# The FFN's down-projection: four passes over 22 chunks, or seven products over 11 pairs of chunks

## The chip, the cores and the metric

The kernel runs on one core of a Trainium2 chip. The metric is the device time of one execution in microseconds (us), the median of several runs. The engines are PE (TensorE, the matmuls; PEld is its weight loads), DVE (VectorE), ACT (ScalarE), POOL (GpSimd) and SP (SyncE, which here issues the transfers by DMA).

## The reference

One layer of a hybrid encoder, on 2048 tokens of 1024 channels in float32. Attention and pooling come first; the change concerns the second half of the layer, with DFF = 2816:

```python
def conv_ffn(x, conv_w, conv_b, w_up, w_down):
    h = x @ w_up
    h = lax.conv_general_dilated(h, conv_w[:, None, :], window_strides=(1,),
                                 padding=[(CONV_WIDTH - 1, 0)],
                                 dimension_numbers=('NWC', 'WIO', 'NWC'),
                                 feature_group_count=2 * D_FF) + conv_b
    gate, val = jnp.split(h, 2, axis=-1)
    return (jax.nn.silu(gate) * val) @ w_down
...
        ffn = conv_ffn(x, conv_w[l], conv_b[l], w_ffn_up[l], w_ffn_down[l])
        x = layer_norm(ALPHA * x + ffn, ln2_g[l], ln2_b[l])
```

## The kernel before

A float32 product is emulated: each operand is split into `hi` (rounded to fp32r, on ACT) and `lo` (the rest, on DVE or POOL), and `mm3` issues three matmuls, hi·hi, hi·lo and lo·hi. Tokens are worked on in two halves of 1024. `ffn` (L1669) runs `up_half(0)`, `down_half(0)`, `up_half(1)`, `down_half(1)` one after the other.

**Up-projection.** `up_half` (L1463) has 22 units of 7 steps: each unit makes 256 channels, for 1024 tokens, by seven products of sums and differences of blocks (`ORDER`), 12 matmuls in a step. Evacuations add and subtract the products from PSUM into small tiles (`m`, eight buffers of 2 KB a partition). Two units in a row are gate and value of the same channels; a pair of units yields two chunks of h. Beside the next unit run the steps of `conv` (L1501): two multiply-adds per chunk on DVE, and in `hidden` (L1526) the product with the gate, after which the chunk of 128 channels x 1024 tokens (512 KB) goes to `self.store`; `turn` (L346) issues it on SP a step later (L353). In the first half, POOL and ACT also build the block sums of the up weights (`up_weights`), stored by the same way and fetched with `up_fetch` (L1459). DVE also makes sums of x (`x_mix`, L1409).

**Down-projection.** `down_half` (L1594) runs four passes per token half: two quarters of 512 tokens (q) by two halves of the outputs (c), each over the 22 chunks of h (k), so 88 steps. A step loads a block of h and a block of the weights, 256 KB each, into the two halves of one tile (`down_load`, L1579, transfers at L1582 and L1583), splits it in `down_split` (L1585), and issues 12 matmuls, three for each of four token blocks of 128 rows, which add up in four PSUM banks (`p1`). Loads run one step ahead of the split, splits two steps ahead of the matmuls; the first three loads and two splits are made in the last unit of the up-projection. After a pass, DVE adds each bank into a tile y that came from memory (512 KB, L1640); after c = 1 the tile is normed (`norm_stages`: ACT sums, DVE and POOL small operations, two DVE operations of 128x1024) and stored. In the fourth pass of the first half, `x_load`, `x_turn` and `x_mix` of the second half are called by a table in `ffn` (`ahead_up`, steps 1 to 21 of the pass). The last six chunks of the very last pass are held and worked off bank by bank.

The Tile framework gives out the buffers (`b`: 42 of 4 KB a partition, `m`: 8 of 2 KB, PSUM `p1`: 4 banks, `p2`: two pairs of banks) and the waits; on each engine instructions run in the order in which they were placed. Every engine instruction passes a helper that counts work, so its line in the profile is L140 and tiles tell the instructions apart; transfers keep their own lines.

## Time and profile before

| | us |
|---|---|
| median of 3 runs | 3350.85 (3349.14 to 3353.66) |
| profiled execution, its own time | 3344.69 |
| its span, first to last instruction | 3342.9 |
| mean granted TensorE clock, share of full | 0.984 |
| first up-projection, by the trace | 1960 to 2403 |
| first down-projection | 2403 to 2666 |
| second up-projection | 2666 to 3087 |
| second down-projection | 3087 to 3343 |

A time of the profiled execution is set against 3344.69, not against the median. Busy shares overlap, since the engines run side by side; an engine's idle time costs something only where a later one waits for it. PE's matmuls are pipelined, so the distance between their starts counts, not the length of one.

### The profile page before, as it was taken

Reading aid. Unit: us, or ns where it says so; the run is one execution under the profiler, and the core shown is the slowest. Engines: PE = TensorE matmul, PEld = TensorE weight load, DVE = VectorE, ACT = ScalarE, POOL = GpSimd, SP = SyncE. Lnnn points to the kernel's source line nnn. Section 1 sums busy time; section 2 is a strip of 40 time slices with the busy share of each in tenths; the row PEclk is TensorE's granted clock in tenths of the full one; section 3 lists DMA queues with packets and bytes.
Section 4 is the critical chain, followed back from the end, with each engine's and each line's share of the span. In section 5 each row is a group of like instructions: output and inputs, shape, how many; then the busy total and the mean of one; then the engine's idle time right before and its main releaser. Section 6 shows DMA issues by size and latency. Waiting matters only on the chain.

```text
span 3342.9 us, 47116 instructions
## 1 busy us (share of the span) xinstructions
PE 3213.2 (96%) x16182; PEld 2703.1 (81%) x16182; DVE 2326.4 (70%) x4378; ACT 1606.5 (48%) x2876; POOL 1208.8 (36%) x1269
## 2 busy tenths in 40 slices
PE   8998899999999899999999989999999999999998
PEld 8887688888898788888788877778788788888787
DVE  5589878996899887777676665565555755555655
ACT  3455837855777666666511133332354522223542
POOL 3139400010011786766631165440185500000754
PEclk9999899999999999999999999999999999999999
DMA  8457755753665444344464378986587466655763
GB/s 322 145 196 277 258 196 199 252 186 136 225 248 186 138 168 160 142 167 154 162 219 154 127 259 322 333 330 221 208 291 238 158 239 232 225 210 208 268 219 130
DMA packets 300334, 711.11 MB, mean 213 GB/s; under 512 B 27258, under 2 KB 112190, under 8 KB 300094
## 3 DMA queue, kind: packets, MB, share of 16 engines
q1 hardware_dynamic: 290302, 690.26, 57.9%
q10 hardware_dynamic: 9792, 17.83, 1.4%
q8 instruction: 128, 2.10, 0.3%
q14 instruction: 112, 0.92, 0.1%
HBM read 497.06 MB, written 210.93 MB: 212 GB/s over the span
## 4 chain that ended last, share of the span: by engine, by line
PE 55%; DVE 5%; issue 2%; POOL 1%; ACT 1%; DMA 1%; SPq 0%; POOLq 0%; DVEq 0%; ACTq 0%
PE p L140 55%; DVE b L140 4%; ACT b L140 1%; DVE m L140 1%; POOL b L140 1%; DMA b<-in_w_ffn_down_dram 0%; DMA h<-b 0%; DMA b<-uw 0%; ACT m L140 0%; POOL lt L140 0%; POOL nr L140 0%; POOL l L140 0%; POOL lr L140 0%; POOL lv L140 0%; DVE nt L140 0%
## 5 line engine op out<-in xcount | busy, mean ns | idle before, releaser
L140 PE MATMUL p<-b,b 128*128 128x512 f32 (+2 forms) x12820 | 2843.3, 369 | 65.5 <-ACT b L140 21.8
L140 PEld LDWEIGHTS p<-b,b 128*128 128x128 f32 x12820 | 2206.4, 191 | 471.6 <-ACT b L140 23.9
L140 POOL TENSOR_TENSOR b<-b,b 128x512 fp32r<-128x512 f32 (+3 forms) x408 | 529.4, 1318 | 690.2 <-DMA b<-x 408.1
L140 ACT ACTIVATE b<-p 128x512 fp32r<-128x512 f32 (+9 forms) x726 | 428.5, 612 | 652.3 <-PE p L140 617.7
L140 ACT ACTIVATE b<-b 128x1024 fp32r<-128x1024 f32 (+2 forms) x270 | 275.8, 1029 | 354.3 <-DMA b<-in_w_ffn_down_dram 138.0
L140 ACT ACTIVATE m<-b,F 128x448 bf16<-128x448 f32 (+3 forms) x448 | 366.0, 819 | 80.7 <-DVE F L140 70.8
L140 DVE TENSOR_TENSOR b<-b,b 128x512 fp32r<-128x512 f32 (+4 forms) x268 | 320.0, 1220 | 102.4 <-ACT b L140 78.9
L140 DVE TENSOR_SCALAR_CACHE_REDUCE m<-b,F 128x512 bf16<-128x512 f32 (+6 forms) x476 | 370.9, 809 | 15.5 <-DMA q<-m 10.6
L140 DVE TENSOR_TENSOR m<-m,p 128x512 f32<-128x512 f32 x176 | 120.6, 685 | 271.4 <-ACT b L140 207.0
L140 PE MATMUL p<-b 128*128 128x512 f32 x704 | 271.3, 390 | 0.4 <-DVE b L140 0.4
L140 DVE SCALAR_TENSOR_TENSOR b<-b,cw,b 128x1023 f32<-128x1023 f32 (+1 forms) x176 | 248.4, 1413 | 30.6 <-ACT b L140 28.9
L140 POOL TENSOR_SCALAR b<-b 128x256 fp32r<-128x256 f32 (+3 forms) x216 | 117.7, 559 | 370.6 <-DMA b<-in_w_in_dram 168.1
L140 DVE TENSOR_TENSOR b<-p,b 128x512 fp32r<-128x512 f32 (+1 forms) x286 | 201.5, 713 | 60.1 <-ACT b L140 57.8
L140 PE MATMUL p<-ident,b 128*128 128x128 f32 x1456 | 213.7, 275 | 20.8 <-ACT b L140 14.2
L140 DVE CUSTOM_DVE_ANT_0 b<-p,b 128x1024 f32<-128x1024 f32 (+7 forms) x192 | 174.0, 908 | 67.0 <-PE p L140 65.5
L140 PEld LDWEIGHTS p<-ident,b 128*128 128x128 f32 x1456 | 175.4, 142 | 53.7 <-ACT b L140 17.5
L140 ACT ACTIVATE b<-b,mx 128x1024 f32<-128x1024 f32 (+7 forms) x192 | 171.6, 896 | 67.7 <-DVE mx L140 63.4
L140 ACT ACTIVATE m<-p 128x512 f32<-128x512 f32 (+1 forms) x180 | 105.5, 594 | 177.8 <-PE p L140 164.7
L140 DVE SCALAR_TENSOR_TENSOR b<-b,ws,b 128x768 f32<-128x768 f32 (+5 forms) x154 | 157.4, 1050 | 41.7 <-ACT b L140 39.4
L140 PEld LDWEIGHTS p<-b 128*128 128x128 f32 x704 | 132.1, 188 | 28.5 <-DVE b L140 1.2
L140 PE MATMUL p<-kst,b 128*128 128x384 f32 (+3 forms) x656 | 150.4, 359 | 4.5 <-DVE b L140 3.3
L140 ACT ACTIVATE b<-m 128x512 fp32r<-128x512 f32 x138 | 82.8, 624 | 131.0 <-DVE m L140 98.4
(122 smaller groups left out, 2174.9 us busy)
## 6 DMA issues: line engine op xcount, KB each, us to landing
b<-uw SPq DMA_DIRECT2D x308, 512.0 KB, 6.2
b<-wp SPq DMA_DIRECT2D x192, 512.0 KB, 6.0
uw<-l SPq DMA_DIRECT2D x98, 512.0 KB, 2.7
b<-h SPq DMA_DIRECT2D x176, 256.0 KB, 5.3
b<-in_w_ffn_down_dram SPq DMA_DIRECT2D x176, 256.0 KB, 5.4
wp<-b SPq DMA_DIRECT2D x64, 512.0 KB, 5.8
uw<-b SPq DMA_DIRECT2D x56, 512.0 KB, 4.3
b<-in_w_ffn_up_dram SPq DMA_DIRECT2D x44, 512.0 KB, 6.2
```

The source lines that it names most:

```text
L140: return f(*args, **kw)
```

## The change

A half of the down-projection becomes seven products (`DOWN`). The operands are quartered: h by token quarter t and by even or odd chunk j, the weights by even or odd chunk j and by output half c. Each product runs over 11 pairs of chunks, so 77 steps a half. Five products take a sum or difference of two blocks of h (`H_SUMS`), five a sum or difference of two weight blocks (`V_SUMS`), and each product is added into one or two quarters of y (`PARTS_OF`).

- h is stored as 77 blocks of 256 KB a half: two plain versions and five sums for each pair. `total` forms the sums in a small tile, on DVE in the first half and on POOL in the second, one in each step of the following unit. The last pair's blocks are stored without a step's delay (`keep_h`, L1599).
- For a sum of weights `down_load` loads two blocks, one into a small tile, and `down_split` adds them on POOL; `lo` is then one DVE operation of 128x1024. For the two plain products the split is as before.
- The banks of a product alternate between `p1` and `p2` (in the first half `p1` alone from the fifth on, with the last two steps of the fifth and sixth held). Collects go from 16 to 48 a half. All eight y tiles load in the first product. Token quarter 1 is normed after product 6, quarter 0 after product 7. Loads run one step further ahead.
- The table for the second half's x now applies to the last two products (5 and 7) of the first half.

```diff
+DOWN = (4, 2, 1, 3, 6, 5, 7)
+H_PLAIN = {3: (0, 0), 4: (1, 1)}
+H_SUMS = {1: ((0, 0), (1, 1), OP.add), 2: ((0, 1), (1, 1), OP.add), 5: ((0, 0), (1, 0), OP.add),
+          6: ((0, 1), (0, 0), OP.subtract), 7: ((1, 0), (1, 1), OP.subtract)}
+V_PLAIN = {2: (0, 0), 5: (1, 1)}
...
+PARTS_OF = {4: ((1, 0, OP.add), (0, 0, OP.add)), 2: ((1, 0, OP.add), (1, 1, OP.subtract)),
+            1: ((0, 0, OP.add), (1, 1, OP.add)), 3: ((0, 1, OP.add), (1, 1, OP.add)), 6: ((1, 1, OP.add),),
+            5: ((0, 1, OP.add), (0, 0, OP.subtract)), 7: ((0, 0, OP.add),)}
...
-                    self.store(self.d_h[hf][2 * p + i - 1], a[i])
+                    for m, (j, t) in H_PLAIN.items():
+                        if j == i - 1:
+                            self.keep_h(hf, m, p, a[i][:, t * G:(t + 1) * G], p == NF // 2 - 1)
+                    if i == 1:
+                        for m in DOWN:
+                            if m in H_SUMS:
+                                self.hsum.append(lambda m=m: total(m))
+
+            def total(m):
+                (j0, t0), (j1, t1), op = H_SUMS[m]
+                s = self.M([P, G])
+                engine = nc.vector if hf == 0 else nc.gpsimd
+                engine.tensor_tensor(s, a[j0 + 1][:, t0 * G:(t0 + 1) * G], a[j1 + 1][:, t1 * G:(t1 + 1) * G], op=op)
+                self.keep_h(hf, m, p, s, p == NF // 2 - 1)
...
+                if self.hsum:
+                    self.hsum.pop(0)()
...
     def down_load(self, hf, i):
+        m, p = DOWN[i // (NF // 2)], i % (NF // 2)
+        t = self.T([P, 2, G])
...
+        if m in V_PLAIN:
+            weights(t[:, 1], V_PLAIN[m])
+            s = None
+        else:
+            u, v, _ = V_SUMS[m]
+            s = self.M([P, G])
+            weights(t[:, 1], u)
+            weights(s, v)
+        self.nc.sync.dma_start(t[:, 0], self.d_h[hf][m][p])
...
     def down_split(self, i):
...
+        if s is not None:
+            nc.gpsimd.tensor_tensor(t[:, 1], t[:, 1], s, op=V_SUMS[m][2])
         hi, lo = self.T([P, 2, G], F32R), self.T([P, 2, G], F32R)
         nc.scalar.activation(hi, t, AF.Copy)
-        nc.vector.tensor_tensor(lo[:, 0], t[:, 0], hi[:, 0].bitcast(F32), op=OP.subtract)
-        nc.gpsimd.tensor_tensor(lo[:, 1], t[:, 1], hi[:, 1].bitcast(F32), op=OP.subtract)
+        if s is not None:
+            nc.vector.tensor_tensor(lo, t, hi.bitcast(F32), op=OP.subtract)
+        else:
+            nc.vector.tensor_tensor(lo[:, 0], t[:, 0], hi[:, 0].bitcast(F32), op=OP.subtract)
+            nc.gpsimd.tensor_tensor(lo[:, 1], t[:, 1], hi[:, 1].bitcast(F32), op=OP.subtract)
...
     def down_half(self, hf):
...
+        def collect(m, r, ps):
+            for t, c, op in PARTS_OF[m]:
+                y = ys[t * RB + r][:, c * G:(c + 1) * G]
+                if (t, c, r) in fresh:
+                    nc.vector.tensor_tensor(y, y, ps, op=op)
+                else:
+                    fresh.add((t, c, r))
+                    nc.vector.scalar_tensor_tensor(y, y, ALPHA, ps, op0=OP.mult, op1=op)
+
+        for mi, m in enumerate(DOWN):
+            if mi % 2 == 0 or hf == 0 and mi >= 4:
                 acc = [self.PS1() for _ in range(RB)]
...
+            lastk = LASTK if final else 2 if hf == 0 and mi in (4, 5) else 0
...
+                if mi == 0 and 1 <= p <= 8:
+                    b = (p + 3) % 8
+                    y = ys[b] = self.T([P, D])
+                    nc.sync.dma_start(y, self.d_x1[hf][b])
...
+                if hf == 0 and mi >= 5:
+                    for f in self.ahead_up.get(i - 5 * NP, ()):
+                        f()
```

**DVE, from the first up-projection to the first down-projection.** Before: `cw` marks the convolution's multiply-adds, `b<-b,b 128x1024` its product with the gate, `b<-b,b 128x512` the `lo` of a step's h.

```order
L140 SCALAR_TENSOR_TENSOR b_25605<-b_25523,cw_21918,b_25605 128x1022
L140 TENSOR_TENSOR b_25621<-b_25594,b_25620 128x512
L140 TENSOR_TENSOR b_25605<-b_25605,b_25455 128x1024
L140 TENSOR_TENSOR b_25645<-b_25602,b_25644 128x512
L140 SCALAR_TENSOR_TENSOR b_25652<-b_25537,cw_21918,b_25652 128x1023
L140 TENSOR_TENSOR b_25668<-b_25625,b_25667 128x512
L140 SCALAR_TENSOR_TENSOR b_25652<-b_25537,cw_21918,b_25652 128x1022
L140 TENSOR_TENSOR b_25652<-b_25652,b_25491 128x1024
L140 TENSOR_TENSOR b_25690<-b_25649,b_25689 128x512
```

Now: the rows that end in `m_...` are the sums of h of the last pair; `b_25907` and `b_25875` are its two chunks.

```order
L150 TENSOR_TENSOR b_25928<-b_25870,b_25927 128x1024
L150 SCALAR_TENSOR_TENSOR b_25907<-b_25796,cw_22028,b_25907 128x1022
L150 TENSOR_TENSOR b_25907<-b_25907,b_25746 128x1024
L150 TENSOR_TENSOR b_25956<-b_25892,b_25955 128x1024
L150 TENSOR_TENSOR m_25964<-b_25907,b_25875 128x512
L150 TENSOR_TENSOR b_25983<-b_25902,b_25982 128x1024
L150 TENSOR_TENSOR m_25991<-b_25907,b_25875 128x512
L150 TENSOR_TENSOR b_26010<-b_25931,b_26009 128x1024
L150 TENSOR_TENSOR m_26018<-b_25907 128x512
L150 TENSOR_TENSOR m_26043<-b_25907,b_25875 128x512
L150 TENSOR_TENSOR m_26068<-b_25875 128x512
```

The `lo` of a step is twice as wide, and five sums (both operands of two of them lie in one chunk) stand between the `lo` of the first product.

**SP, at the same place.** Before, two stores of h (L353) stand among the loads (L1582 of h, L1583 of weights):

```order
L1583 DMA b_25649<-in_w_ffn_down_dram 128x512
L353 DMA h_204<-b_25605 128x1024
L1582 DMA b_25672<-h_190 128x512
L1583 DMA b_25672<-in_w_ffn_down_dram 128x512
L1582 DMA b_25694<-h_191 128x512
L1583 DMA b_25694<-in_w_ffn_down_dram 128x512
L353 DMA h_203<-b_25652 128x1024
L1582 DMA b_25715<-h_192 128x512
```

Now (L1599 direct store of h, L1617 weights, L1627 h, L1709 y):

```order
L1599 DMA h_226<-b_25907 128x512
L1617 DMA b_25959<-in_w_ffn_down_dram 128x512
L1617 DMA m_25960<-in_w_ffn_down_dram 128x512
L1627 DMA b_25959<-h_191 128x512
L1599 DMA h_204<-m_25964 128x512
L1709 DMA b_25967<-x_181 128x1024
L1617 DMA b_25986<-in_w_ffn_down_dram 128x512
L1617 DMA m_25987<-in_w_ffn_down_dram 128x512
L1627 DMA b_25986<-h_192 128x512
L1599 DMA h_215<-m_25991 128x512
L1709 DMA b_25994<-x_181 128x1024
```

Each step's loads have a store and a y tile of 512 KB ahead of them, and the store waits for the DVE row that makes its block.

**DVE, from the first to the second product.** Now: `b<-b,p` are collects, `b_25912` and so on the y tiles, `p_6531` and so on the banks, `b<-b,b` the `lo`. The last three `lo` of the first product come first:

```order
L150 TENSOR_TENSOR b_26037<-b_25959,b_26036 128x1024
L150 TENSOR_TENSOR b_26062<-b_25986,b_26061 128x1024
L150 TENSOR_TENSOR b_26087<-b_26013,b_26086 128x1024
L150 SCALAR_TENSOR_TENSOR b_25912<-b_25912,p_6531_25856 128x512
L150 SCALAR_TENSOR_TENSOR b_26021<-b_26021,p_6531_25856 128x512
L150 SCALAR_TENSOR_TENSOR b_25940<-b_25940,p_6532_25857 128x512
L150 TENSOR_TENSOR b_26108<-b_26040,b_26107 128x512
L150 SCALAR_TENSOR_TENSOR b_26046<-b_26046,p_6532_25857 128x512
L150 SCALAR_TENSOR_TENSOR b_25967<-b_25967,p_6533_25858 128x512
```

Before, at the end of the first pass:

```order
L140 TENSOR_TENSOR b_26040<-b_26004,b_26039 128x512
L140 SCALAR_TENSOR_TENSOR b_25630<-b_25630,p_6368_25590 128x512
L140 SCALAR_TENSOR_TENSOR b_25740<-b_25740,p_6369_25591 128x512
L140 SCALAR_TENSOR_TENSOR b_25843<-b_25843,p_6370_25592 128x512
L140 SCALAR_TENSOR_TENSOR b_25945<-b_25945,p_6371_25593 128x512
L140 TENSOR_TENSOR b_26068<-b_26024,b_26067 128x512
```

Four collects have become eight, and the `lo` of the second product's first step (`b_26108`) stands behind three of them.

## Rows read from the trace of the kernel before

**Rows 1.** The page's first part: busy time of each engine, its share of the span, and instructions:

```profile
PE 3213.2 (96%) x16182; PEld 2703.1 (81%) x16182; DVE 2326.4 (70%) x4378; ACT 1606.5 (48%) x2876; POOL 1208.8 (36%) x1269
```

**Rows 2.** Busy time by stretch: the first up-projection, the first down-projection, the second up-projection, the second down-projection. Columns: start and end, length, busy time of each engine with its instructions, granted TensorE clock, busy share of the DMA engines, GB/s:

```profile
1960.00:2403.00 443.00, 421.56 (x1786) 339.39 (x1785) 248.96 (x244) 149.64 (x230) 152.33 (x112) 0.97 0.81 297
2403.00:2666.00 263.00, 257.20 (x1157) 210.94 (x1155) 171.47 (x185) 124.88 (x149) 167.67 (x104) 1.00 0.63 216
2666.00:3087.00 421.00, 419.20 (x1810) 338.71 (x1811) 236.14 (x338) 120.26 (x140) 6.57 (x4) 0.99 0.62 227
3087.00:3343.00 256.00, 241.78 (x1060) 198.04 (x1058) 155.76 (x177) 107.56 (x114) 150.01 (x95) 0.98 0.58 201
```

**Rows 3.** The chain of TensorE's weight loads (PEld) in the first down-projection (2403 to 2666 us): what they waited for, us in total, times, longest:

```profile
PEld p L140 <- DVE b L140: 5.2, 6, 1.1
PEld p L140 <- POOL b L140: 1.5, 2, 1.0
```

**Rows 4.** The same in the end of the second up-projection and the second down-projection (3080 to 3343 us):

```profile
PEld p L140 <- DVE b L140: 3.5, 4, 2.0
PEld p L140 <- POOL b L140: 1.6, 2, 1.2
```

**Rows 5.** The same in the first up-projection (1960 to 2403 us), and below the dots the longest item among the waits of SP's DMA queue (1940 to 2380 us):

```profile
PEld p L140 <- DVE m L140: 13.7, 18, 5.4
PEld p L140 <- DVE b L140: 9.2, 3, 5.2
PEld p L140 <- DMA b<-uw: 6.3, 2, 4.3
PEld p L140 <- ACT m L140: 2.2, 10, 0.2
...
SPq L353 <- POOL b L140: 144.4, 47, 6.9
```

**Rows 6.** The timeline of PE in the first down-projection: start, length, what, how many in the row:

```profile
2440.54 0.39 PE L140 MATMUL p<-b 128*128 128x512 f32 x1
2440.77 0.62 PE L140 MATMUL p<-b,b 128*128 128x512 f32 x2
2441.22 0.39 PE L140 MATMUL p<-b 128*128 128x512 f32 x1
```

**Rows 7.** The timelines of DVE and of POOL in the first down-projection: a DVE and a POOL operation that each had the start of the other, then both engines at once (POOL: three operations in the row):

```profile
2498.60 0.69 DVE L140 TENSOR_TENSOR b<-b,b 128x512 fp32r<-128x512 f32 x1 [1.96 <-PE p L140]
...
2526.60 1.29 POOL L140 TENSOR_TENSOR b<-b,b 128x512 fp32r<-128x512 f32 x1 [15.66 <-ACT b L140]
...
2640.29 1.79 DVE L140 TENSOR_TENSOR b<-b,b 128x512 fp32r<-128x512 f32 x1
...
2639.78 5.14 POOL L140 TENSOR_TENSOR b<-b,b 128x512 fp32r<-128x512 f32 x3
```

**Rows 8.** Groups of DVE instructions by form in the second up-projection (2700 to 3050 us), where POOL is idle: out<-in, shapes, count, busy us, mean ns, idle before:

```profile
L140 DVE TENSOR_TENSOR b<-b,b 128x1024 f32<-128x1024 f32 x18 | 21.2, 1220 | 0.0
```

**Rows 9.** Groups of instructions by form in the first down-projection, same columns: POOL's and DVE's `lo`, DVE's `lo` of the mixed x, the collects from PSUM, the five forms of a norm on DVE, and the transposes on PE:

```profile
L140 POOL TENSOR_TENSOR b<-b,b 128x512 fp32r<-128x512 f32 x87 | 143.0, 1669 | 52.2 <-ACT b L140 38.8 <-PE p L140 8.0 <-DVE b L140 3.6
...
L140 DVE TENSOR_TENSOR b<-b,b 128x512 fp32r<-128x512 f32 x87 | 96.9, 1142 | 40.3 <-ACT b L140 30.9 <-PE p L140 7.5 <-DMA b<-x 1.0
...
L140 DVE TENSOR_TENSOR b<-m,b 128x512 fp32r<-128x512 f32 x12 | 17.8, 1500 | 0.0
...
L140 DVE SCALAR_TENSOR_TENSOR b<-b,p 128x512 f32<-128x512 f32 x16 | 10.8, 687 | 34.4 <-PE p L140 34.4
...
L140 DVE SCALAR_TENSOR_TENSOR b<-b,nr,b 128x1024 f32<-128x1024 f32 x6 | 7.7, 1284 | 0.2
L140 DVE SCALAR_TENSOR_TENSOR b<-b,nm,b 128x1024 f32<-128x1024 f32 x6 | 7.6, 1274 | 0.0
L140 PE MATMUL p<-ident,b 128*128 128x128 f32 x64 | 7.6, 273 | 0.0
...
L140 DVE SCALAR_TENSOR_TENSOR nt<-nr,nv 128x1 f32<-128x1 f32 x6 | 5.4, 905 | 2.3 <-POOL nr L140 2.3
...
L140 DVE TENSOR_TENSOR nr<-nr,nt 128x1 f32<-128x1 f32 x6 | 1.9, 310 | 0.2
...
L140 DVE TENSOR_SCALAR nt<-nt 128x1 f32<-128x1 f32 x6 | 0.9, 152 | 0.2
```

**Rows 10.** The timeline of DVE at the start of the first down-projection (brackets: idle time before the row, and what ended it):

```profile
2404.03 3.15 DVE L140 TENSOR_TENSOR b<-b,b 128x512 fp32r<-128x512 f32 x2
2407.11 4.55 DVE L140 SCALAR_TENSOR_TENSOR b<-b,cw,b 128x1023 f32<-128x1023 f32 x2
2411.58 4.61 DVE L140 TENSOR_TENSOR b<-b,b 128x512 fp32r<-128x512 f32 x3
...
2419.22 1.83 DVE L140 TENSOR_TENSOR b<-b,b 128x1024 f32<-128x1024 f32 x2
2423.16 0.69 DVE L140 TENSOR_TENSOR b<-b,b 128x512 fp32r<-128x512 f32 x1 [2.12 <-ACT b L140]
```

**Rows 11.** Two short stretches of the first up-projection, columns as in rows 2:

```profile
1972.00:1976.00 4.00, 0.90 (x4) 0.40 (x3) 3.10 (x5) 1.24 (x1) 3.20 (x7) 1.00 1.03 413
...
1977.00:1983.00 6.00, 5.14 (x12) 4.07 (x13) 4.84 (x5) 0.95 (x1) 2.58 (x2) 0.50 0.94 335
```

**Rows 12.** The fourth pass of the first down-projection, in which the next half's x is mixed, columns as in rows 2:

```profile
2586.00:2652.00 66.00, 64.38 (x313) 52.90 (x313) 47.60 (x44) 30.62 (x44) 39.58 (x24) 1.00 0.55 177
```

More of the change, by code (lines that the diff above doesn't have):

```diff
@@ L442, in setup @@
         self.d_x1 = [self.DT([NB // 2, P, D], name="x1") for _ in range(2)]
[L443 removed]
+        self.d_h = [{m: [self.DT([P, G], name="h") for _ in range(NF // 2)] for m in DOWN} for _ in range(2)]
         self.I = {}
@@ L1570, in up_more, with keep_h @@
             next(self.wgen, None)
+    def keep_h(self, hf, m, p, src, now):
+        if now:
+            self.nc.sync.dma_start(self.d_h[hf][m][p], src)
+        else:
+            self.store(self.d_h[hf][m][p], src)
     def down_ahead(self, hf, step):
@@ L1607, in norm @@
             norm_tick()
[L1609 to L1614 removed]
+        NP = NF // 2
+        total = len(DOWN) * NP
         gb = self.load_norm("ln2_g", "ln2_b")
         loaded, split = 3, 2
[L1617 to L1633 removed]
+        ys, fresh = {}, set()
@@ new lines, in product @@
+        def product(acc, p, r, part):
+            hi, lo = part
+            c = slice(r * P, (r + 1) * P)
+            self.mm3(acc[r], hi[:, 0, c], lo[:, 0, c], hi[:, 1], lo[:, 1], p == 0, p == NP - 1)
+        def collect(m, r, ps):
[3 more added lines that the diff above has]
+                    nc.vector.tensor_tensor(y, y, ps, op=op)
+                else:
+                    fresh.add((t, c, r))
+                    nc.vector.scalar_tensor_tensor(y, y, ALPHA, ps, op0=OP.mult, op1=op)
@@ new lines, in down_half @@
+        for mi, m in enumerate(DOWN):
+            if mi % 2 == 0 or hf == 0 and mi >= 4:
+                acc = [self.PS1() for _ in range(RB)]
+            else:
+                t = [self.PS2([P, 2, G]) for _ in range(2)]
+                acc = [t[0][:, 0], t[0][:, 1], t[1][:, 0], t[1][:, 1]]
+            final = hf == 1 and mi == len(DOWN) - 1
+            lastk = LASTK if final else 2 if hf == 0 and mi in (4, 5) else 0
+            held = []
+            for p in range(NP):
+                i = mi * NP + p
+                ahead = 2 + max(0, p - 2) if final else 2
+                while split < min(i + 1 + ahead, total):
+                    if loaded < min(split + 3, total):
@@ L1634, in down_half @@
                         self.down_load(hf, loaded)
                         loaded += 1
-                    if k in self.pending:
-                        self.pending.pop(k)()
-                    if c == 0 and k % 5 == 1 and len(ys) < RB:
-                        y = self.T([P, D])
-                        nc.sync.dma_start(y, self.d_x1[hf][q * RB + len(ys)])
-                        ys.append(y)
-                    part = self.dparts.pop(i)
-                    if final and k >= NF - LASTK:
-                        held.append((k, part))
-                    else:
-                        for rb in range(RB):
-                            down(acc, k, rb, part)
@@ L1648, in down_half @@
-                    if hf == 0 and q == 1 and c == 1:
-                        for f in self.ahead_up.get(k, ()):
-                            f()
-                    norm_tick()
-                    if not held:
-                        yield 2.7
-                for rb in range(RB):
-                    for k, part in held:
-                        down(acc, k, rb, part)
-                    nc.vector.scalar_tensor_tensor(ys[rb][:, cs], ys[rb][:, cs], ALPHA, acc[rb], op0=OP.mult, op1=OP.add)
-                    if c == 1:
-                        norm((hf * 2 + q) * RB + rb, ys[rb], TAIL[rb] if final else "A--")
-                    if held:
-                        yield 2.7
+                    self.down_split(split)
@@ new lines, in down_half @@
+                part = self.dparts.pop(i)
+                if p >= NP - lastk:
+                    held.append((p, part))
+                else:
+                    for r in range(RB):
+                        product(acc, p, r, part)
+                if hf == 0 and mi >= 5:
+                    for f in self.ahead_up.get(i - 5 * NP, ()):
+                        f()
+                norm_tick()
+                if not held:
+                    yield 2.7
+            for r in range(RB):
+                for p, part in held:
+                    product(acc, p, r, part)
+                collect(m, r, acc[r])
+                for t in (1,) if m == 6 else (0,) if m == 7 else ():
+                    norm(hf * 2 * RB + t * RB + r, ys.pop(t * RB + r), TAIL[r] if final else "A--")
+                if held:
+                    yield 2.7
```

46 lines of the change are left out of this document (19 added, 27 removed).

## The prediction

> **What bounds the kernel now.** The page's first part first: TensorE (PE) is busy for 96% of the span, the vector engine DVE for 70%, GpSimd (POOL) for 36% [rows 1]. Then the span cut at the four stages of the FFN, the only part that changes [rows 2]: in all four PE is busy for 94% or more, so matmuls set the pace and other work matters where PE waits. Last, where it waits: 6.7 us for DVE and POOL in the first down-projection [rows 3], 5.1 us in the second [rows 4], but 31 us in the first up-projection, where DMA moves 297 GB/s and POOL and DVE feed the weight sums [rows 2, 5].
>
> **Matmuls removed.** A step of the down-projection is 12 matmuls in both kernels; a half had 88 steps and has 77. Three matmuls start every 0.68 us [rows 6], 0.2267 us each. 2 x 11 x 12 = 264 fewer: **-59.8 us**, if nothing else becomes the pace.
>
> **The steady step.** 55 of a half's 77 steps now load 768 KB instead of 512 (289 GB/s over 2.72 us), add two weight blocks on POOL, and make `lo` in one DVE operation of 128x1024 where it had been 128x512 on DVE and the same on POOL. Prices: POOL 128x512 takes 1.29 us alone and 1.71 beside DVE; DVE 128x512 takes 0.69 alone and 1.79 beside POOL [rows 7], so a meeting costs DVE 1.1. The 128x1024 form takes 1.22 alone [rows 8]; its bound beside POOL is 1.22 + 1.1 = 2.32. ACT's part is unchanged. The collects from PSUM go from 16 to 48 a half at 0.69 [rows 9]: 33 us, 0.43 a step. So DVE has 1.65 to 2.75 us a step against PE's 2.72. I cost the steady step at nothing, since the upper end needs every pair to meet. At present DVE's 128x512 averages 1.14 us and POOL's 1.67 [rows 9]: (1.14 - 0.69)/1.1 = 41% of DVE's extra and (1.67 - 1.29)/0.42 = 90% of POOL's. The cover is DVE's idle time, 91 of 263 us in the first down-projection and 100 of 256 in the second [rows 2].
>
> [...]
>
> **From up to down.** In the order, the first steps' `lo` (now 128x1024) stand among the tail of the convolution, and five new sums stand there too; on SP the loads of the steps from the eighth on stand behind direct stores that wait for those DVE results. Now DVE runs without a pause from 2404.03 to 2421.05 us, then idles 2.1 of each 2.7 us [rows 10], and PE still waits 5.2 us for it in this half [rows 3]: the lead is already used. Added: about seven of the `lo` double, 7 x (1.22 - 0.69) = 3.7, and five sums of 0.69 to 1.79, 3.5 to 9: 7 to 13 us. If the idle time behind absorbs all of it the cost is 0; if none, some 10. I take **+5**, the middle, since the lead of two steps (5.4 us) can take about half. In the second half the sums are POOL's, but they lock DVE and hold the same loads; **+5** again, bounds 0 to 10. DMA: 11 x 0.786 MB and eight y tiles of 0.524 MB are 12.8 MB in the first product's 29.9 us, 430 GB/s where a short stretch shows 413 [rows 11]: 1.2 us late, inside this term.
>
> **First to second product.** The `lo` of the second product's first step stands behind three collects. The first collect can start 0.68 us into the last step, 2.04 before it ends; 3 x 0.69 + 0.69 to 1.79 = 2.75 to 3.85: 0.7 to 1.8 late. I take 1.5 a half, **+3**. At the other boundaries five or more `lo` stand ahead of the collects; nothing.
>
> **The stretch where the next half's x is mixed** (end of the first down-projection). DVE is busy 47.6 of 66 us there now [rows 12], beside POOL. Added: eleven `lo` double (5.8), eight collects more (5.5), and four norms, moved in from the pass before: each two operations of 1.28, one of 0.91, one of 0.31 and three of 0.15 [rows 9]: 4.2 x 4 = 16.9. That is 75.8 us against 66: 10 over. If DVE's operations there ran alone (the sixteen `lo` at 0.69 instead of 1.14, the twelve of x at 0.69 instead of 1.50 [rows 9]), some 17 us less, nothing is over. Bounds 0 and 20; I take **+10**.
>
> **Up-projections.** Stores of h go from 22 of 512 KB to 77 of 256 KB a half: 8.65 MB more, 20 GB/s on 297. In the first half DVE makes 55 sums: 38 to 98 us on 249 [rows 2], 15 to 39%. [...] I take **+5**, nearest the cheap sum, as DVE has 44% idle there. In the second half POOL makes them; it is busy 6.6 of 421 us, DVE 236 [rows 2]: 0. If the cover goes, 55 meetings of 1.1 still fit DVE's idle time.
>
> **Sum.** -59.8 + 10 + 3 + 10 + 5 = -31.8. The profiled execution took 3344.69 us (span 3342.9), 6.2 under the median of 3350.85; 3344.7 - 31.8 = 3312.9, and with the 6.2 **3319 us**. All lower ends together: -58.4, 3292; all upper: 20 + 3.6 + 20 + 20 - 59.8 = +3.8, 3355.
>
> **Rivals.**
> A, nearly the full gain: DVE's idle time covers the transitions and the mixing, some 8 us go. For it: DVE idles a third of the time; against it: its idle time lies elsewhere than the new work. -51.8: 3299.
>
> B, DVE and POOL lock each other until DVE paces the down-projections. DVE alone in the first: 55 x 1.22 + 22 x 0.69 + 48 x 0.69 + 8 x 4.2 + 29 of x at 0.69 = 169 us, PE 77 x 2.72 + 7.6 of transposes [rows 9] = 217; 87 POOL operations cost up to 1.1 each, 96. It decides from half of them meeting (48). With 80% it is 246, 29 over; in the second half 149 + 68 = 217 against 209, 8 over. In place of the two terms of +10: -59.8 + 37 + 8 = -14.8, 3336. Against it is the 41%; for it, the 90%. [...]
>
> C, slower: the sums in the first up-projection hold buffers. A sum keeps one of the eight small buffers, from which evacuations of PSUM also draw, until its store has landed, and its store queues on SP, which waits 144.4 us in 47 waits there for POOL's weight sums [rows 5], 3.1 each. If PE loses such a wait, it is 34 us over the 11 pairs of units: the break-even is about one a pair. With two a pair, 68 in place of 5: 3319 + 63 = 3382. Against it: DVE has slack, and evacuations come 2.7 us apart; for it, PE's longest waits are already on DVE's `m` tiles, 5.4 us [rows 5].
>
> That the change doesn't do what it says can be left out: the order has the 264 fewer matmuls.
>
> **How the numbers follow.** A measurement here tells 0.2%, 6.7 us: faster is below 3344, slower above 3358. Forecast 0.50, A 0.17, B 0.20 (a quarter of it, with over 90% meeting, near no change), C 0.10, the upper ends together 0.03. Faster 0.50 + 0.17 + 0.15 = 0.82, same 0.05 + 0.03 = 0.08, slower 0.10. The range from 3296 to 3348 takes in A's centre and most of B and leaves out C and the tips.
>
> **What would show it.** In the profile after: 264 fewer matmuls; down-projections of about 250 and 233 us instead of 263 and 256, with PE's waits on DVE at their start and in the mixing; the first product's DMA above 400 GB/s; the DVE `lo` of 128x1024 at 1.3 to 2.3 us. DVE without idle time through a whole down-projection would be B; a first up-projection some 30 us longer than 443, C; down-projections of 240 and 229 us or less, A. I am wrong if the loss lies in a stage that I cost at nothing, above all the second up-projection.

## The result and the profile after

The changed kernel took 3334.23 us (median of 8 runs, 3323.26 to 3339.07) against 3349.99 for the kernel before (8 runs beside it): a ratio of 0.9948, 95% interval 0.9933 to 0.9964. That is some 16 us faster where 32 were forecast; the time lies inside the range, on its slow side, nearer to the centre of rival B (3336) than to the forecast's own 3319. The profiled execution took 3325.95 us, its span 3324.2, 18.7 shorter than the span before.

The page's first part, to set against [rows 1]:

```profile
PE 3168.4 (95%) x15918; PEld 2658.2 (80%) x15918; DVE 2423.5 (73%) x4475; ACT 1585.2 (48%) x2854; POOL 1271.3 (38%) x1302
```

The 264 matmuls are gone (16182 to 15918). The four stages, in the columns of [rows 2], cut at the first matmul of each but for the first, which starts at 1960 as there:

```profile
1960.00:2413.50 453.50, 424.31 (x1787) 339.09 (x1785) 283.30 (x294) 148.47 (x229) 158.51 (x114) 0.97 0.84 302
2413.50:2666.30 252.80, 236.65 (x1024) 188.95 (x1024) 208.47 (x213) 115.81 (x140) 157.54 (x93) 0.97 0.77 272
2666.30:3087.70 421.40, 419.39 (x1813) 338.64 (x1814) 236.56 (x338) 120.57 (x140) 70.23 (x55) 1.00 0.65 241
3087.70:3324.20 236.50, 215.37 (x925) 175.01 (x923) 187.60 (x198) 95.96 (x102) 152.76 (x88) 0.97 0.75 266
```

The first up-projection lost 10 us, the first down-projection (263.6 before, from its first matmul) gained 10.8, the second up-projection is unchanged, the second down-projection (255.3) gained 18.8. Each down-projection was due 29.9 for its matmuls, so 19.1 and 11.1 us were given back. Where, three stretches of the first (the start, the steady middle, the mixing of x to the end of the stage) and two of the second (the start, the middle) tell:

```profile
2413.50:2475.50 62.00, 55.30 (x219) 41.33 (x220) 48.81 (x43) 24.88 (x24) 33.26 (x21) 0.97 0.94 345
2475.50:2588.50 113.00, 113.00 (x507) 93.50 (x506) 98.29 (x94) 52.02 (x57) 80.85 (x45) 1.00 0.77 275
2588.50:2666.10 77.60, 68.36 (x301) 54.12 (x299) 61.17 (x76) 38.71 (x58) 43.43 (x28) 0.93 0.63 209
3087.60:3149.70 62.10, 53.00 (x210) 40.83 (x209) 40.42 (x41) 24.04 (x23) 39.46 (x24) 0.95 0.91 326
3149.70:3277.70 128.00, 128.00 (x566) 106.03 (x565) 113.51 (x105) 59.28 (x64) 98.03 (x54) 1.00 0.81 280
```

The same places before the change, the first start, the mixing and the second start:

```profile
2402.92:2464.97 62.05, 60.38 (x262) 48.67 (x262) 41.25 (x33) 35.17 (x34) 49.97 (x31) 1.00 0.78 273
2577.97:2666.34 88.37, 83.89 (x398) 68.76 (x396) 64.22 (x72) 40.54 (x61) 49.66 (x32) 1.00 0.52 171
3087.55:3149.60 62.05, 59.74 (x260) 48.26 (x260) 39.28 (x37) 35.14 (x34) 48.33 (x31) 1.00 0.77 271
```

In the steady stretches, the second and the last, PE never waits: 113 of 113 us and 128 of 128. At the first start, in the mixing of x and at the second start it idles 6.7, 9.2 and 9.1 us (2.8 of the 9.2 are the wait at the end of the stage, which was there before), and the granted clock falls from 1.00 to 0.97, 0.93 and 0.95. One less the clock, times the length, is 1.9, 5.4 and 3.1 us: by this estimate of mine the most that the clock can have cost there. It is not simply to be added, since PE would have waited in part of that time at either clock: at the first start of the same kernel's second profile (a0_again) the clock stood at 1.00, and 62.05 us held no more matmuls.

```profile
2417.36:2479.41 62.05, 53.62 (x219) 39.98 (x220) 48.76 (x43) 24.92 (x24) 33.47 (x21) 1.00 0.93 341
```

What PE's weight loads waited for in the first down-projection, to set against [rows 3]; ACT now works behind POOL's sum of weights, and 3.2 of its 8.6 us are the wait at the end of the stage, which [rows 3] does not take in:

```profile
PEld p L150 <- DVE b L150: 12.5, 12, 2.4
PEld p L150 <- ACT b L150: 8.6, 5, 3.2
PEld p L150 <- POOL b L150: 3.5, 5, 1.1
```

The timeline of PE in the mixing, and the clock behind its gap:

```profile
2609.62 0.61 PE L150 MATMUL p<-b,b 128*128 128x512 f32 x2
2613.08 0.47 PE L150 MATMUL p<-b 128*128 128x512 f32 x1 [2.85 <-DVE b L150]
...
2617.49 0.80 PE L150 MATMUL p<-b 128*128 128x512 f32 x1 [1.66 <-DVE b L150]
```

```profile
2613.80:2620.60 6.80, 5.08 (x11) 3.02 (x11) 6.80 (x9) 0.36 (x1) 4.84 (x3) 0.50 1.08 349
```

After 2.85 us without a matmul the granted clock was 0.50 for 6.8 us. The kernel before has 6 us at 0.50 as well, 1 us after a stretch of 4 us with PE busy for 0.90 of them [rows 11]. Not every gap is followed so: after the waits of 1.50 and 1.66 us before the matmuls at 2430.53 and 2435.20, at the first start, the clock stayed at 1.00 (2425 to 2452 us).

PE's weight loads in the first up-projection, and SP's longest waits there, against [rows 5]:

```profile
PEld p L150 <- DMA b<-uw: 17.9, 8, 5.1
PEld p L150 <- DVE m L150: 11.4, 15, 5.4
PEld p L150 <- DVE b L150: 8.4, 7, 3.0
```

```profile
SPq L363 <- POOL b L150: 136.6, 46, 8.2
SPq L363 <- DVE b L150: 53.7, 12, 11.0
SPq L363 <- DVE m L150: 44.6, 23, 8.7
SPq L1471 <- PE p L150: 23.2, 17, 6.5
```

By what ended PE's waits, those for DVE have not grown, and those for fetches of up weights have, from 6.3 to 17.9 us (the runs below show that this alone is not the loss). SP has a new item, stores that wait for DVE's sums (44.6), while its own lead, the time in which a fetch waits for PE to free a buffer, shrank to 23.2 us (71.5 before).

### The profile page after: what moved, and what is told of

Its sections match the earlier page's. It is cut to its first block, busy times and chain, and to the rows that moved or that the text cites. A ratio compares the mean times of both kernels' runs of the same rounds, so it can differ in the third digit from the quotient of the medians.

```text
span 3324.2 us, 46905 instructions
## 1 busy us (share of the span) xinstructions
PE 3168.4 (95%) x15918; PEld 2658.2 (80%) x15918; DVE 2423.5 (73%) x4475; ACT 1585.2 (48%) x2854; POOL 1271.3 (38%) x1302
## 5 line engine op out<-in xcount | busy, mean ns | idle before, releaser
L150 PE MATMUL p<-b,b 128*128 128x512 f32 (+3 forms) x12644 | 2785.6, 369 | 79.5 <-ACT b L150 20.6
L150 PEld LDWEIGHTS p<-b,b 128*128 128x128 f32 x12644 | 2173.6, 191 | 484.0 <-ACT b L150 23.1
L150 ACT ACTIVATE b<-p 128x512 fp32r<-128x512 f32 (+9 forms) x726 | 428.7, 612 | 667.9 <-PE p L150 628.1
L150 ACT ACTIVATE b<-b 128x1024 fp32r<-128x1024 f32 (+2 forms) x248 | 253.2, 1027 | 397.7 <-POOL b L150 148.9
L150 DVE TENSOR_TENSOR b<-b,b 128x1024 fp32r<-128x1024 f32 (+5 forms) x246 | 358.6, 1488 | 78.9 <-ACT b L150 75.9
L150 ACT ACTIVATE m<-b,F 128x448 bf16<-128x448 f32 (+3 forms) x448 | 366.1, 820 | 84.2 <-DVE F L150 67.3
L150 DVE TENSOR_SCALAR_CACHE_REDUCE m<-b,F 128x512 bf16<-128x512 f32 (+6 forms) x476 | 370.8, 808 | 17.8 <-DMA q<-m 12.4
L150 POOL TENSOR_TENSOR b<-b,b 128x256 fp32r<-128x256 f32 (+3 forms) x276 | 315.9, 1161 | 72.3 <-ACT b L150 66.2
L150 DVE TENSOR_TENSOR m<-m,p 128x512 f32<-128x512 f32 x176 | 120.5, 685 | 245.2 <-ACT b L150 207.0
L150 POOL TENSOR_TENSOR b<-b,m 128x512 f32<-128x512 f32 x110 | 196.7, 1808 | 237.9 <-DMA b<-h 165.3
L150 POOL TENSOR_TENSOR m<-b,b 128x512 f32<-128x512 f32 x99 | 144.4, 1466 | 349.4 <-issue 258.4
L150 DVE SCALAR_TENSOR_TENSOR b<-b,cw,b 128x1023 f32<-128x1023 f32 (+1 forms) x176 | 243.4, 1385 | 35.7 <-ACT b L150 34.5
L150 POOL TENSOR_SCALAR b<-b 128x256 fp32r<-128x256 f32 (+3 forms) x216 | 117.3, 558 | 379.4 <-DMA b<-in_w_in_dram 127.7
L150 PE MATMUL p<-b 128*128 128x512 f32 x616 | 235.8, 399 | 13.2 <-ACT b L150 8.7
L150 DVE TENSOR_TENSOR b<-p,b 128x512 fp32r<-128x512 f32 (+1 forms) x286 | 201.5, 713 | 59.5 <-ACT b L150 57.2
L150 PE MATMUL p<-ident,b 128*128 128x128 f32 x1456 | 214.8, 277 | 20.9 <-ACT b L150 14.4
L150 DVE CUSTOM_DVE_ANT_0 b<-p,b 128x1024 f32<-128x1024 f32 (+7 forms) x192 | 173.9, 908 | 67.4 <-PE p L150 66.1
L150 PEld LDWEIGHTS p<-ident,b 128*128 128x128 f32 x1456 | 176.6, 142 | 53.5 <-ACT b L150 17.5
L150 ACT ACTIVATE b<-b,mx 128x1024 f32<-128x1024 f32 (+7 forms) x192 | 171.6, 896 | 67.2 <-DVE mx L150 63.0
L150 DVE SCALAR_TENSOR_TENSOR b<-b,ws,b 128x768 f32<-128x768 f32 (+5 forms) x154 | 157.4, 1050 | 43.1 <-ACT b L150 41.0
L150 ACT ACTIVATE m<-p 128x512 f32<-128x512 f32 (+1 forms) x180 | 105.4, 593 | 152.9 <-PE p L150 136.9
L150 PE MATMUL p<-kst,b 128*128 128x384 f32 (+3 forms) x656 | 151.6, 361 | 4.5 <-DVE b L150 3.3
## 6 DMA issues: line engine op xcount, KB each, us to landing
b<-in_w_ffn_down_dram SPq DMA_DIRECT2D x154, 256.0 KB, 5.4
b<-h SPq DMA_DIRECT2D x154, 256.0 KB, 5.4
h<-m SPq DMA_DIRECT2D x110, 256.0 KB, 5.6
```

The source lines that it names most:

```text
L150: return f(*args, **kw)
```

## The experiments

Every kernel is the changed one with one or two edits, the last two with three. Whole times scatter, and the stages before the FFN, the same program in all but b2_m10, end up to 17 us apart from one execution to the next; the stages of the FFN agree better, so they carry the verdicts. Stage lengths in us from one profile each: first up-projection from its first gap on, then the other three.

| run | median us | ratio to before, 95% interval | up 1 | down 1 | up 2 | down 2 |
|---|---|---|---|---|---|---|
| kernel before | 3349.99 | | 425.1 | 263.6 | 421.1 | 255.3 |
| changed kernel | 3334.23 | 0.9948 (0.9933 to 0.9964) | 435.1 | 252.8 | 421.3 | 236.5 |
| a0_again | 3329.55 | 0.9948 (0.9931 to 0.9964) | 438.8 | 254.6 | 421.4 | 235.4 |
| a1_late_sums | 3325.12 | 0.9934 (0.9912 to 0.9955) | 436.2 | 250.7 | 421.4 | 233.0 |
| a2_no_sums | 3318.00 | 0.9917 (0.9899 to 0.9936) | 426.4 | 254.2 | 421.7 | 236.3 |
| a3_no_norms | 3330.38 | 0.9955 (0.9939 to 0.9972) | 434.8 | 253.5 | 421.4 | 236.0 |
| b0_later_stores | 3324.46 | 0.9936 (0.9917 to 0.9956) | 430.4 | 253.0 | 421.5 | 236.0 |
| b1_late_all | 3330.70 | 0.9948 (0.9932 to 0.9963) | 438.4 | 252.1 | 421.5 | 234.0 |
| b2_m10 | 3335.49 | 0.9964 (0.9950 to 0.9979) | 432.8 | 253.1 | 421.1 | 234.6 |
| b3_no_weight_add | 3317.42 | 0.9907 (0.9881 to 0.9933) | 435.4 | 243.2 | 421.8 | 230.0 |
| c0_add_aside | 3336.02 | 0.9957 (0.9942 to 0.9973) | 433.9 | 256.0 | 421.4 | 235.6 |
| c1_no_sum_stores | 3325.31 | 0.9925 (0.9903 to 0.9947) | 422.9 | 258.1 | 421.5 | 234.6 |
| c2_vsum_late | 3349.44 | 1.0006 (0.9993 to 1.0019) | 431.2 | 249.5 | 459.3 | 224.2 |
| d0_plain_late | 3331.04 | 0.9940 (0.9924 to 0.9957) | 429.1 | 255.5 | 421.7 | 237.9 |

**The same kernel again.** 

> The changed kernel unaltered, for a second profile. The four stages of the first one (first up-projection from 1960 us to the first matmul of the down-projection 453.5 us, first down-projection 252.8, second up-projection 421.4, second down-projection 236.5) should come again within 3 us each if the losses belong to the program; a first up-projection that is 6 us or more off would mean that its 10 us are mostly scatter of one execution.

Three stages come again within 2 us; the first up-projection is 4 us longer, a little beyond the 3 expected. In the seven profiles that leave it as it is, it takes 433.9 to 438.8 us against 425.1 before (one profile), so some 10 us belong to the program.

### What the first up-projection lost

**Without the sums, same bytes.**

```diff
             def total(m):
                 (j0, t0), (j1, t1), op = H_SUMS[m]
+                if hf == 0:
+                    self.keep_h(hf, m, p, a[j0 + 1][:, t0 * G:(t0 + 1) * G], p == NF // 2 - 1)
+                    return
```

> In the first half the sums of h are left out; a plain block of the same size is stored in the place of each, so the bytes are the same, DVE is spared 55 operations and SP doesn't wait for them. Theory D (DVE's sums delay the evacuations of the first up-projection): that stage falls by 8 us or more, to 445 or less. Theory B (the 8.65 MB of added stores delay the fetches of up weights): it stays within 3 us of 453. In between (3 to 8 us) the stores' waits for DVE on SP's queue would be the larger part.

426.4 us: all but 1.3 us come back, so the bytes alone cost next to nothing. Theory D's figure is met; but whether DVE's time, SP's wait for DVE or the small tiles that the sums hold were saved, this run can't tell. PE's waits for fetches of up weights are as long as in the changed kernel (`PEld p L150 <- DMA b<-uw: 17.2, 7, 5.1`), though the loss is gone: late fetches alone are not the loss.

**With the sums, without their stores.** The down-projection reads a plain block instead of each but the last pair's.

```diff
+                if hf == 0 and p < NF // 2 - 1:
+                    return
                 self.keep_h(hf, m, p, s, p == NF // 2 - 1)
...
-        self.nc.sync.dma_start(t[:, 0], self.d_h[hf][m][p])
+        self.nc.sync.dma_start(t[:, 0], self.d_h[hf][m if hf or m in H_PLAIN or p == NF // 2 - 1 else 3][p])
```

> In the first half the sums of h are made but, but for the last pair's, not stored; the down-projection reads a plain block in the place of each. DVE's work stays, 13 MB of stores and SP's waits for the sums go. From the first gap of the first up-projection to the down-projection it was 435 to 439 us in the changed kernel, 426 without the sums, 430 with the stores two steps later. Theory S (SP's order and the bytes): 428 or less. Theory E (DVE's sums themselves): 433 or more. Between them both have a part.

422.9 us: DVE makes every sum (271.6 us busy, 268.5 in the changed kernel) and nothing is lost there; the first down-projection is longer, 258.1 us, so that both stages together take 681.0, as without the sums (680.6), against 687.9 and 693.4 in the changed kernel. So DVE's work alone is free, the bytes alone are nearly free, and only a sum that is also stored costs. Such a store waits on SP for its sum, and the sum holds its small tile until the store has landed (in the changed kernel POOL waits twice for such a store, `POOL m L150 <- DMA h<-m: 10.8, 2, 7.2`); here both fall away. SP's waits in the two runs, of this one first:

```profile
SPq L363 <- POOL b L150: 145.1, 47, 7.9
SPq L1471 <- PE p L150: 61.6, 26, 6.5
SPq L363 <- DVE b L150: 55.6, 9, 11.0
```

```profile
SPq L363 <- POOL b L150: 131.0, 45, 8.5
SPq L363 <- DVE b L150: 51.5, 11, 11.1
SPq L1471 <- PE p L150: 45.1, 27, 6.6
```

In both SP's lead is mostly back (61.6 and 45.1 us of waiting for PE), and the stores' waits for DVE's small tiles are gone but for 2.0 us.

**Stores two steps later.**

```diff
         else:
-            self.store(self.d_h[hf][m][p], src)
+            self.after(2, lambda: self.store(self.d_h[hf][m][p], src))
```

> The queued stores of h (plain blocks and sums) are issued two steps later, when the sum has long been made; the sums and the bytes stay. Theory S (in the first up-projection the fetches of up weights stand on SP behind stores that wait for DVE's sums): from the first gap of that stage to the first matmul of the down-projection, 425 us before the change and 435 to 439 after, it falls to 430 or less, and SP's waits at the stores for DVE's small tiles, 44.6 us, fall below 15. Theory E (the sums themselves delay DVE's evacuations, or hold the small buffers): it stays at 434 or more, and with buffers held longer it could grow.

430.4 us, at the edge of theory S's figure, and 429.1 and 431.2 in the two last runs that share the edit: some 5 of the 10 us come back. Its other figure fails, since SP still waits 40 us for the sums (`SPq L363 <- DVE m L150: 40.3, 18, 8.3`), and its lead has not come back either (18.2 us of waiting for PE). So SP's standing at these stores is not shown to be the cost. Ten small tiles (below) gave 432.8 us, 1 to 6 under the seven profiles of the changed stage: a part of the tiles is not ruled out. What links the stored sums to the 10 us stays open.

### What the down-projections gave back

**Late sums, and late stores as well.** In the second kernel the plain blocks' direct stores also go some steps later.

```diff
-                elif self.hsum:
+                elif self.hsum and mi > 0:
                     self.hsum.pop(0)()
```

> The five sums of the last pair of chunks are formed from the second product on, instead of in the first, so that neither their DVE or POOL work nor their stores stand among the first product's loads. Theory Q (the start of a down-projection loses its time to SP's order: loads behind stores that wait for the sums): each down-projection is 4 to 6 us shorter, 248 and 231. Theory L (the start loses its time to DVE and POOL locking each other, and to the rate of the transfers): 0 to 2 us shorter each.

```diff
         if now:
-            self.nc.sync.dma_start(self.d_h[hf][m][p], src)
+            self.after({4: 2, 3: 6}.get(m, 1), lambda: self.nc.sync.dma_start(self.d_h[hf][m][p], src))
```

> As the run with late sums, and the last pair's two plain blocks are also stored some steps later, just ahead of the loads that need them. Theory Q (the start loses its time to SP's order): both down-projections are 6 us or more shorter than in the changed kernel, 247 and 230 or less, 3 below the run with late sums (250.7 and 233.0). If what is left at the start is the tail of the convolution on DVE and the wider operation, it stays within 1.5 us of that run.

The late sums bring 2 to 4 us in the first and 2.4 to 3.5 in the second, between the theories' figures; the plain blocks' later stores nothing more (252.1, 234.0). At the first start of the changed kernel SP stands 10.8 us at those two direct stores until DVE has the chunk, with loads behind them; with late stores that is 2.5 us, and PE waits for DVE instead, 8.1 us in all. So the last pair's sums, their work and their stores together, are some 3 us a half; taking the rest of SP's order away gives nothing more.

**Without the four norms of the mixing.**

```diff
+                    if hf == 0 and t == 1:
+                        self.store(self.out[0, (RB + r) * P:(RB + r + 1) * P, :], ys.pop(RB + r))
+                        continue
                     norm(...)
```

> The four norms that run in the stretch where the next half's x is mixed are left out (those four y tiles are stored unnormed). If the forecast's reading of that stretch is right (DVE has 76 us of work for 66), the first down-projection is 8 to 11 us shorter, 242 to 245, and the waits between 2605 and 2645 us go. If the lock of DVE with POOL in the sums of x and weights is what costs there, it is at most 3 us shorter.

253.5 us, no change, though DVE has 14 us less to do (194.7 us busy, 208.5 in the changed kernel), and the waits stay. In the changed kernel the four norms were over by 2590 us, ahead of the first operation on x (2591.8) and of the waits, and in the 66 us from the start of product 5 (2575.9 to 2641.9) DVE was busy 56.6 us, not 75.8. The forecast's sum for that stretch had the right size for a wrong reason: it is not DVE's total work that is too much.

**Ten small buffers.** 

> Ten small buffers instead of eight, 41 big ones instead of 42. Theory M (in the mixing of the next half's x the second weight blocks wait on SP for small tiles that the sums of x hold): the first down-projection is 5 us or more shorter, 249 or less, and SP's waits at the weight loads between 2590 and 2645 us, some 20 us, fall by half. If the lock of DVE and POOL costs there, 252 to 255 as in the changed kernel. In the first up-projection M would give 2 to 5 us back too.

```diff
-        self.big = ctx.enter_context(tc.tile_pool(name="big", bufs=42))
-        self.mid = ctx.enter_context(tc.tile_pool(name="mid", bufs=8))
+        self.big = ctx.enter_context(tc.tile_pool(name="big", bufs=41))
+        self.mid = ctx.enter_context(tc.tile_pool(name="mid", bufs=10))
```

253.1 us: theory M falls for the mixing.

**Without POOL's additions; and with them, but to no one.**

```diff
-            nc.gpsimd.tensor_tensor(t[:, 1], t[:, 1], s, op=V_SUMS[m][2])
+            pass
```

> Both weight blocks are loaded, but POOL's 110 additions of them are left out; DVE's operation of 128x1024 and the bytes stay. Theory L (DVE and POOL lock each other): the operation of 128x1024 falls to about 1.25 us, and the first down-projection is 8 us or more shorter (245 or less), the second 5 or more (231 or less). If the bytes, SP's order and the small buffers make the losses, the two are at most 3 us shorter.

```diff
-            nc.gpsimd.tensor_tensor(t[:, 1], t[:, 1], s, op=V_SUMS[m][2])
+            nc.gpsimd.tensor_tensor(s, t[:, 1], s, op=V_SUMS[m][2])
```

> POOL's 110 additions of weight blocks are made, on the same operands and in the same places, but into a tile that nobody reads; ACT's and DVE's operations take a loaded block alone and don't wait for POOL. The sums of the weights are so left out of the result, as in the run without the additions (243.2 and 230.0 us for the two down-projections against 253 to 255 and 235 to 237). Theory L (POOL's reads lengthen DVE's operations): the mean of the 128x1024 operation stays near 1.65 us and the stages stay within 3 us of the changed kernel. Theory C (the addition is one more link between the transfer and the matmul, 1.3 to 1.8 us in a chain that is only two steps ahead): the stages fall to 246 and 232 or less though the mean stays high.

Without the additions the two stages are 10 and 6 us shorter. That alone could be the lengthening of DVE's operations beside POOL's or the link in the chain. With the additions made aside the link is gone too, and not a microsecond comes back (256.0, 235.6). Without the additions the small tiles also come free sooner, but two more of them had brought nothing (253.1). The groups by form in the first down-projection, of the changed kernel, of the run without additions, and of the one aside:

```profile
L150 POOL TENSOR_TENSOR b<-b,m 128x512 f32<-128x512 f32 x54 | 96.8, 1810 | 33.2 <-DMA m<-in_w_ffn_down_dram 16.6 <-DMA b<-in_w_ffn_down_dram 10.4 <-issue 3.6
L150 DVE TENSOR_TENSOR b<-b,b 128x1024 fp32r<-128x1024 f32 x55 | 93.8, 1745 | 19.7 <-ACT b L150 19.5
```

```profile
L150 DVE TENSOR_TENSOR b<-b,b 128x1024 fp32r<-128x1024 f32 x55 | 67.7, 1266 | 21.9 <-ACT b L150 19.0 <-PE p L150 2.9
```

```profile
L150 POOL TENSOR_TENSOR m<-b,m 128x512 f32<-128x512 f32 x55 | 102.2, 1881 | 192.3 <-DMA b<-in_w_ffn_down_dram 169.9 <-DMA m<-in_w_ffn_down_dram 16.5 <-issue 4.6
L150 DVE TENSOR_TENSOR b<-b,b 128x1024 fp32r<-128x1024 f32 x55 | 99.9, 1862 | 15.1 <-ACT b L150 15.1
```

DVE's operation takes 1.27 us on average without POOL's additions and 1.75 to 1.86 with them, whether or not anyone needs the result: theory L. What it calls a lock is, as far as these runs show, this lengthening. Where that costs, the same stretches of the run without additions show (first start, mixing, second start):

```profile
2408.28:2470.33 62.05, 57.14 (x237) 43.59 (x238) 47.24 (x47) 28.94 (x28) 18.08 (x11) 1.00 1.02 373
2583.33:2651.31 67.98, 61.42 (x283) 49.55 (x281) 54.45 (x69) 35.98 (x54) 23.06 (x16) 0.97 0.70 230
3073.27:3135.32 62.05, 56.92 (x238) 43.52 (x238) 43.22 (x45) 28.04 (x27) 28.49 (x16) 1.00 0.94 347
```

Length less matmuls at 0.2267 us is some 3.9, 5.5 and 6.6 us shorter there than in the changed kernel: POOL's additions cost where no lead is left, at the starts and in the mixing. In the steady stretches they cost nothing, though DVE is busy 87 to 89% of them.

**Additions in the second up-projection.** The late sums, the later stores, and this:

```diff
+                if hf == 1 and (u * 7 + s) % 2 == 1:
+                    self.vsum((u * 7 + s) // 2)
...
+    def vsum(self, k):
+        todo = [(m, p) for m in DOWN if m in V_SUMS for p in range(NF // 2)]
+        if 0 < k <= len(todo):
+            m, p = todo[k - 1]
+            t = self.vt
+            self.nc.gpsimd.tensor_tensor(t[:, 0], t[:, 0], t[:, 1], op=V_SUMS[m][2])
+            self.store(self.d_v[m][p], t[:, 0])
...
+        elif hf == 1:
+            self.nc.sync.dma_start(t[:, 1], self.d_v[m][p])
+            s = None
```

> A version with three changes: the weight sums that the second half needs are made by POOL in the second up-projection, where it is nearly idle, and stored, so that the second down-projection loads one block a step and POOL adds nothing there; the last pair's sums come from the second product on; queued stores of h go two steps later. If POOL's additions cost what the run without them showed, the second down-projection falls from 235 to 237 us to 230 or less (with the late sums 228), the second up-projection stays within 3 us of 421.4, the first down-projection is 2 to 3 us shorter, and the first up-projection 6: in all some 3314 us against 3330 to 3334 for the changed kernel. If the pace of the transfers or the wider operation costs there, the second down-projection stays at 233 or more, and the whole at 3320 or more.

The second down-projection does what theory L promised and more: 224.2 us, under the 225.4 that the matmuls alone would leave. With no additions, late sums and one block less to load a step, its start is at full pace again (263 matmuls in 62.05 us; 260 before the change). But the second up-projection, where I had taken POOL's idle time for free, is 38 us longer:

```profile
2406.60:2656.10 249.50, 234.52 (x1024) 188.43 (x1024) 211.21 (x213) 115.91 (x140) 162.66 (x93) 0.98 0.78 275
2656.10:3115.40 459.30, 430.17 (x1812) 344.66 (x1813) 253.43 (x338) 114.94 (x140) 144.50 (x108) 0.97 0.86 319
3115.40:3339.60 224.20, 210.49 (x925) 173.06 (x923) 154.43 (x198) 94.71 (x102) 57.98 (x35) 0.98 0.60 208
```

PE waits there 21.6 us for DVE's big tiles in seven waits (`PEld p L150 <- DVE b L150: 21.6, 7, 3.9`), six of them some 43 us apart, a pair of units, and the mean clock is 0.97 instead of 1.00. Which of the three new loads (POOL's additions, 78 GB/s more on DMA, stores on SP that wait for POOL) makes them, was not separated.

**A product without additions first.** With the later stores, and four of five sums late.

```diff
-DOWN = (4, 2, 1, 3, 6, 5, 7)
+DOWN = (2, 4, 1, 3, 6, 5, 7)
...
-                elif self.hsum:
+                elif self.hsum and (mi > 0 or len(self.hsum) == 5):
```

> A version with three changes: product 2, which needs no sum of weights, comes first, so that POOL adds nothing and a step loads 512 KB at the start of each down-projection, where no lead is left; four of the last pair's five sums come from the second product on; queued stores of h go two steps later. If DVE and POOL locking each other costs most where the lead is gone (the start), the first down-projection falls from 253 to 255 us to 247 or less and the second from 235 to 237 to 230 or less, each 3 below the run with late sums alone (250.7 and 233.0); the first up-projection is at 430 to 432 us as with later stores alone; the whole is some 3315 us. If the start loses its time to the convolution's tail and the y tiles instead, the down-projections stay at 250 and 233 and the whole is near 3320.

255.5 and 237.9 us: wrong on both. The first four steps run without a loss; then waits come, in the timeline of PE:

```profile
2434.98 2.07 PE L150 MATMUL p<-b,b 128*128 128x512 f32 x4 [3.35 <-DVE b L150]
2454.32 3.34 PE L150 MATMUL p<-b,b 128*128 128x512 f32 x8 [2.75 <-POOL b L150]
2463.10 0.73 PE L150 MATMUL p<-b,b 128*128 128x512 f32 x2 [1.87 <-DVE b L150]
```

Of the 14 us that the first 216 matmuls lose in the first half against 0.2267 us each, 11 are lost in the first product's 132, and 7 of these before POOL's first addition (at 2451.78). There SP stands 11.9 us at the two direct stores of the last pair, waiting for DVE, and ACT idles 10.8 us until a load of h lands that stands behind them. POOL's `lo` of the plain weights also still runs there beside DVE's. So the run does not tell what the additions cost at the start; it shows that a start without them can lose as much to loads that come late. No version that leaves nothing out beats the changed kernel beyond its interval: the late sums and the later stores, each by itself, are ahead by 4 to 10 us with intervals that overlap.

## Why the prediction was right, and where its sizes failed

- **Matmuls removed: right.** The count and the pace hold: -59.8 us, and in the steady stretches nothing takes it back, as "I cost the steady step at nothing" said. DVE at 1.75 us for the wide operation lies between the 1.22 and 2.32 that were its bounds.
- **Second up-projection: right**, 421.1 to 421.4 us, with POOL's sums beside it.
- **From up to down, and the first boundary: right in place, too small.** 6.5 us a half were forecast; the starts gave back 9.5 and 11.6 (length less matmuls at 0.2267 us: 12.2 us where it was 2.7, 14.7 where it was 3.1). The sum had priced DVE's added work with each doubled `lo` as if alone, and half the lead; it left out POOL's additions as partners of every wide operation there, which cost 3.9 and 6.6 us. The last pair's sums with their stores are some 3 us a half. The rest is not separated, and the rate of the transfers (busy share 0.94 and 0.91 at the starts) was not varied by itself; the first product's DMA, which was to show above 400 GB/s, ran at 291 in its first 29.9 us, with SP standing at stores.
- **The mixing: the size nearly right, the reason wrong.** 10 forecast; length less matmuls rose by 11 us. But DVE had 56.6 us of work in the 66, not 75.8, and without the norms nothing changes: that the size fits is luck. POOL's additions make half of it, since without them it falls by 5.5 us; the other half stays open.
- **The first up-projection: twice the forecast**, 10 instead of 5, and not by DVE's added work, from which the term was taken: the sums alone cost nothing. Only sums that are also stored cost, which is rival C's kind; whether by SP's queue or by the small buffers, C's two halves, is not shown. PE lost some 0.9 us a pair of units, under the one wait of 3.1 at which C put its break-even. No run shows the forecast's 5 us, or the 20 that the sum of the upper ends has for it: in the seven profiles the stage was 8.8 to 13.7 us longer than in the one before, at a mean clock of 0.97 in the changed kernel as before it.
- **Rival B** was the nearest to the time (3336) but not the case: it had DVE as the pace of whole stages, and PE never waits in their steady stretches (113 of 113 us, 128 of 128). POOL's additions cost where the lead is gone: of no use to anyone, they cost 18 us over both halves (256.0 and 235.6 against 243.2 and 230.0). B had up to 1.1 us for each of POOL's operations; in the changed kernel the wide operation took 0.48 more on average (1.75 for 1.27).

In sum, in the profiled executions some 40 us of the gain were given back instead of 28: 10 for 5, 21 for 13, 11 for 10, less 2 in the rest of the two stages. The terms that were too small are the starts (13, measured 21) and the first up-projection (5, measured 10). Both were priced by DVE's added work; the runs show in its place POOL's additions (10.5 of the 21) and sums that are also stored (the last pair's, some 3 a half, and the 10); the rest of the starts stays open.

## What to carry to other kernels

Where an algorithm trades matmuls for additions, the steady loop can hide them (PE busy 113 of 113 us here) and the kernel still lose at the starts, where no lead is left (12.2 and 14.7 us for 2.7 and 3.1); price starts by the lengthened operations (1.75 us for 1.27 here), not by the added ones alone. Work that is free by itself and bytes that are free by themselves can cost together: the sums of h cost 10 us only when they were also stored. Nor is an idle engine's time free for that reason alone: with POOL's additions DVE's wide operation took 1.75 us for 1.27. And where several things arrive late at once, taking one away lets the next one set the time, as the late stores showed: a run that brings nothing does not prove its cause absent.

## What the runs showed of the hardware

In the run with additions in the second up-projection an instruction of one element per partition on DVE lasted until POOL's operation had ended. The timelines of DVE and of POOL there:

```profile
2775.31 1.22 DVE L150 SCALAR_TENSOR_TENSOR b<-hl,cw,b 128x1 f32<-128x1 f32 x1
...
2777.65 0.21 DVE L150 SCALAR_TENSOR_TENSOR b<-hl,cw,b 128x2 f32<-128x2 f32 x1
```

```profile
2774.72 1.80 POOL L150 TENSOR_TENSOR b<-b 128x512 f32<-128x512 f32 x1 [4.27 <-DMA b<-in_w_ffn_down_dram]
```

The first takes 1.22 us and ends with POOL's operation (2776.53 and 2776.52); one of the same form 6 us earlier took 1.25 and ended so too (2770.47 and 2770.45). With POOL idle, from 2776.52 to 2781.02, the larger twin takes 0.21. The collects, which read one operand from PSUM, took 0.68 us on average in the first down-projection of the changed kernel, against 0.69 before [rows 9]; one of them, at 2612.26 us, took 0.67 beside an addition of POOL's (2611.75 to 2613.48).
